# Fixing the first four experts, keeping the split tokens in natural order, and moving the end of the sort into the first experts

## The chip, the cores and the metric

The kernel runs on one core of a Trainium2 chip. The metric is the time of one execution on the device in microseconds (us), the median of several runs. The engines of the core are PE (matrix products; PEld is its weight load, which overlaps the products), DVE, ACT and POOL (elementwise work), and SP, which here only issues transfers (DMA).

## The reference, cut to what matters

The reference is a whole block with two attentions and a mixture of experts, followed by a second block. Only the mixture is touched. Each of 512 tokens picks one of 4 groups, then 2 of the 8 experts of that group; every one of the 32 experts has its own three weight matrices.

```python
pg = jax.nn.softmax((hf @ wg + bg), axis=-1)
gsel = jnp.argmax(pg, axis=-1)
le = (hf @ we + be).reshape(n, N_GROUPS, EXPERTS_PER_GROUP)
le = jnp.take_along_axis(le, gsel[:, None, None], axis=1)[:, 0]
p_top, e_loc = lax.top_k(jax.nn.softmax(le, axis=-1), TOP_K)
gate = pg_sel[:, None] * p_top / jnp.sum(p_top, axis=-1, keepdims=True)
...
def expert_block(args):
    xb, e = args
    return (jax.nn.silu(xb @ w1[e]) * (xb @ w3[e])) @ w2[e]
...
out = jnp.zeros((n + 1, d), ys.dtype).at[tok_buf].add(ys)[:n]
```

d is 1024, the hidden width of an expert 512. One expert's weights are 3 x 2 MB in fp32, all of them 192 MB.

## The kernel before, in words

`phase2` does the output projection of the attention, the routing and the experts. The 512 tokens are four tiles (t = 0 to 3) of 128 rows.

**Routing.** `project` adds the projection to the residual `x`. For each tile, `logits` transposes `x` on PE and multiplies by the router's weights, `route` finds group and experts by a chain of small DVE instructions, and a product with `Ab` gives each token its rank within its expert. `onehot` turns ranks into a selection matrix `G`. `spread` writes the normalized tile as a sum of two rounded parts, `hi` (ACT) and `lo` (DVE), in fp32r; both are written permuted, so that the 128 columns that one product needs stand side by side. For tile 2 `lo` is computed on POOL.

**Order of the experts.** `sort` orders the experts by how many tokens they have; its `key` puts those with a mark of 65536 first. `idi` holds the sorted experts' numbers, `rp` the ranks and gates in that order. `STEPS` says how many experts each of 12 steps takes: 2 (with 64 rows each) or 4 (with 32 rows). Experts 0 and 1 are marked, so that step 0 is known when the program is built.

**Steps.** A gather multiplies `hi` and `lo` (the stationary operand, as `hv(t, b)[:, k * P:(k + 1) * P]`) by `G` and leaves the chosen tokens transposed in `xg`, in 8 blocks k. The first gather, for step 0, stands at line 1141. `expert_step` then does w1 and w3 in halves of 4 blocks, the gate, four transposes and w2; between its parts `todo[0]` to `todo[4]` run what belongs to other steps: gathers ahead (line 1006), the preparation of gates (`slots`), and `back`, which adds the finished step's result to `x` (the combine, line 1304).

**Weights.** The pool behind `slot()` has 14 buffers of 1 MB (`NW2`). A step of two experts takes 12 of them, four for each matrix, a step of four experts 24. SP issues the loads strictly in program order; a load waits until the products that read its buffer's last content are done, and from step 1 on it waits for `value_load`, which reads the experts' numbers from `idi` (line 868). Experts that have more tokens than rows are taken by a loop after the steps; its body does not run with these inputs. The work after the experts (`project2`) begins when the last combine is done.

Of the kernel before, what the change touches and what calls it, by code (L numbers as in the profile page):

```python
# [10 lines left out]
F32 = mybir.dt.float32  # L11
# [3 lines left out]
AF = mybir.ActivationFunctionType  # L15
# [14 lines left out]
def constants():  # L30

    c = {}
    q = np.arange(P)
    c["sq"] = np.concatenate([
        np.eye(P),
        np.where(q[None, :] < q[:, None], 0.0, NEG),
        q[:, None] < q[None, :],
    ], axis=1).astype(np.float32)

    tok = np.arange(S)  # L40
    f = np.float32(10000.0) ** (-np.arange(8, dtype=np.float32) / np.float32(8))
# [12 lines left out]

    e = np.arange(32)
    c["order"] = np.concatenate([31 - e + 65536 * (e < 2), PLACES, np.repeat([128 // n for n in STEPS], STEPS)])
    c["rows"] = np.concatenate([
        q[:, None] % 32 == e[None], (q % 32)[:, None],
        q[:, None] // 32 == np.arange(4)[None], q[:, None] // 64 == np.arange(2)[None],
    ], axis=1).astype(np.float32)  # L60
    c["tok1"] = (q[:, None] + P * np.arange(NT)[None, :] + 1).astype(np.float32)

    rel = np.arange(640) - 127 - 384
    n = np.abs(rel)
    nf = np.maximum(n, 1).astype(np.float32)
    large = 8 + (np.log(nf / np.float32(8)) / np.float32(math.log(128 / 8)) * np.float32(8)).astype(np.int32)
    large = np.minimum(large, 15)
    bucket = np.where(rel > 0, 16, 0) + np.where(n < 8, n, large)
    oh = np.zeros((32, 640), np.float32)
    oh[bucket, np.arange(640)] = 1.0  # L70
    c["onehot"] = oh
    return c
# [35 lines left out]

STEPS = (2, 4, 2, 2, 4, 2, 2, 4, 2, 2, 4, 2)
_small, _large = iter(range(16, 32)), iter(range(16))
PLACES = np.array([next(_small if n == 4 else _large) for n in STEPS for _ in range(n)])

# [1 line left out]
class K:  # L116
# [733 lines left out]
    def phase2(self, p2):  # L850
# [13 lines left out]
        def weights(i):  # L864

            n = STEPS[i]
            if i:
                es = [nc.sync.value_load(idi[:, p:p + 1], min_val=0, max_val=E - 1) for p in range(first[i], first[i + 1])]
            else:
                es = range(n)  # L870
            out = []
            for nm in ("w1", "w3", "w2"):
                if i:
                    src = [I[nm][0, bass.ds(e, 1)].rearrange("o (p k) n -> p (o k) n", p=P) for e in es]
                else:
                    src = [I[nm][0, e].rearrange("(p k) n -> p k n", p=P) for e in es]
# [17 lines left out]
        ws = self.wos  # L894
        hs = [None, None]
        hv = lambda t, b: hs[t // 2][b].rearrange("q a s -> q (a s)")[:, (t % 2) * D:(t % 2 + 1) * D]
        Ab = T([P, NT, E], "Ab", BF16)
        st = T([P, NT, 84], "st")

# [77 lines left out]
        def spread(t, rstd):  # L977

            if hs[t // 2] is None:
                hs[t // 2] = self.half(1 - t // 2)  # L980
            hi, lo = hv(t, 0), hv(t, 1)
            xk = self.x[:, t, :].rearrange("q (p k) -> q k p", k=KD)
            r = lambda b: b.rearrange("q (k p) -> q k p", k=KD)
            sc.activation(r(hi), xk, AF.Copy, scale=rstd)
            if t == 2:
                for h in (slice(0, KD // 2), slice(KD // 2, KD)):
                    xs = T([P, S], "pm").rearrange("q (k p) -> q k p", p=P)
                    gp.tensor_scalar(xs, xk[:, h], rstd, None, ALU.mult)
                    gp.tensor_tensor(r(lo)[:, h], xs, r(hi)[:, h].bitcast(F32), ALU.subtract)
            else:  # L990
                stt(r(lo), xk, rstd, r(hi).bitcast(F32), ALU.mult, ALU.subtract)

        def onehot(G, steps, t, src):

# [7 lines left out]
        def gather(xg, G, ks, m):  # L1002
            for k in ks:
                ps = self.psum()
                for i, (b, t) in enumerate((b, t) for t in range(NT) for b in range(2)):
                    te.matmul(ps[:, :m], hv(t, b)[:, k * P:(k + 1) * P], G[:, t, :m],
                              start=i == 0, stop=i == 2 * NT - 1)
                scaled(xg[:, k, :m], ps[:, :m], k)

# [71 lines left out]

        rstd = [None] * NT
        new_G = lambda: T([P, NT, 4 * CAP], "G", F32R)
        G = new_G()
        for i, (t, n) in enumerate(((0, 0), (0, 1), (1, 0), (1, 1), (2, 1), (3, 1), (2, 0), (3, 0))):
            project(t, n)
            if i in (1, 3, 6, 7):
                rstd[t] = self.rsqrt1(1.0 / D, st[:, t, 0:1], st[:, t, 1:2])
                ps = logits(t)
                route(t, ps, rstd[t])  # L1090
                onehot(G, (0,), t, rt)
        order = sort()
        next(order)
        for t in range(NT):
            spread(t, rstd[t])

        def table():

# [31 lines left out]


        NB, NX = 18, 8
        new_xg = lambda: self.xg().rearrange("p a (b s) -> p (a b) s", b=2)
        xg = new_xg()
        acs = [self.accum() for _ in range(4)] + [self.psum() for _ in range(3)]
        acs.append(self.po.tile([P, 512], F32, tag="o", name=self.name("o")))
        part = lambda k: acs[k][:, :P]
        for t in range(NT):
            for k in range(KD):
                for b in range(2):  # L1140
                    te.matmul(part(k), hv(t, b)[:, k * P:(k + 1) * P], G[:, t, :P], start=t + b == 0, stop=t + b == NT)
        for k in range(KD):
            scaled(xg[:, k, :P], part(k), k)
        next(order)
        _, gc = slots(G, (0,), rt)
        combine, nx, got, over = [], None, [], []
        N = len(STEPS)
        for i in range(N):
            todo = [[] for _ in range(5)]
            j = (i + 1) % 2  # L1150
            ahead = [g for g in (i + 2 - j, i + 3 - j) if g < N] if i else (1, 2)
            if i == 0 or (j == 0 and ahead):
                nx = new_xg()
                G = new_G()
                for t in range(NT):
                    onehot(G, ahead, t, rp)
                sl = slots(G, ahead, rp)
                todo[1].append(lambda s=sl: next(s))
                got = []
                todo[3].append(lambda s=sl, g=got: g.append(next(s)))  # L1160
            if ahead:
                m = P * len(ahead)
                if i == 0:
                    todo[0].append(lambda x=nx, g=G, m=m: gather(x, g, range(4), m))
                k0 = 4 * j
                todo[2].append(lambda x=nx, g=G, k=k0, m=m: gather(x, g, (k, k + 1), m))
                todo[3].append(lambda x=nx, g=G, k=k0, m=m: gather(x, g, (k + 2, k + 3), m))
            for p, f in zip((0, 1), combine):
                todo[p].append(f)
            if i == 1:  # L1170
# [5 lines left out]
            if last:  # L1176
                more = self.next_weights()
                todo[4].append(self.split_next)
            c = 0 if i == 0 else j
            combine = self.expert_step(T, xg, c * P, STEPS[i], P, w1, w3, w2, gc[:, 0, c:c + 1], gc[:, 1, c:c + 1],  # L1180
                                       iota, todo)
            if last:
                for f in combine:
                    f()
            if j and not last:
                xg = nx
                gc, = got

        tab, tabi = over
        _, (nb,) = nc.values_load_multi_w_load_instructions(tabi[:, NB:], min_val=0, max_val=NB)  # L1190
        with tc.For_i(0, nb, 1) as ib:
# [26 lines left out]
            for k in range(KD):  # L1218
                ps = self.psum()
                for i, (b, t) in enumerate((b, t) for t in range(NT) for b in range(2)):  # L1220
                    te.matmul(ps[:, :CAP], hv(t, b)[:, k * P:(k + 1) * P], G[:, t, :CAP],
                              start=i == 0, stop=i == 2 * NT - 1)
# [3 lines left out]
            for f in self.expert_step(T, xg, 0, 1, CAP, w1, w3, w2, gc[:, 0, :1], gc[:, 1, :1], iota):  # L1226
                f()


# [19 lines left out]
        self.split_next = split_next  # L1249
        return self.free  # L1250

    def expert_step(self, T, xg, c0, ne, m, w1, w3, w2, gate, tok, iota, todo=()):


        nc = self.nc
# [8 lines left out]
        for i, (w, a) in enumerate(zip((w1, w3), ac)):  # L1264
# [10 lines left out]
        v.scalar_tensor_tensor(h[:m], ac[1][:m], gate[:m], h[:m], ALU.mult, ALU.mult)  # L1275
        between(2)
        ps = self.psum()
        for k in range(4):
# [5 lines left out]
        v.tensor_scalar(pm[:m], iota[:m], tok[:m], None, ALU.is_equal)  # L1284
        y = [self.accum() for _ in range(2)]
        kp = 4 // len(w2)
        for k in range(4):
# [559 lines left out]
```

## Time and profile before

| what | value |
|---|---|
| time, median of 3 runs | 1518.69 us (1517.68 to 1523.06) |
| profiled execution | 1516.21 us, span 1514.4 us |
| PE busy | 1432.1 us, 95% of the span |
| PEld / DVE / ACT / POOL busy | 962.0 / 720.6 / 502.1 / 123.8 us |
| granted clock of PE, mean | 0.971 of full speed |
| moved by DMA | 303.81 MB, mean 201 GB/s |

The shares are means over stages with different limits: routing and first gather end at about 377 us, the twelve steps run to about 857 us, and there the transfers matter; before and after, the weights are small against the products. [...]

### The profile page before, as it was taken

To read this page: it belongs to the slowest core of one execution; us is meant where nothing else is said; L and a number is where in the kernel's file an instruction comes from. 1 tells how busy PE (TensorE), PEld (TensorE's weight loads), DVE (VectorE), ACT (ScalarE), POOL (GpSimd) and SP (SyncE) were. 2 spreads that over 40 slices of the span, in tenths; PEclk is the share of its full clock that TensorE was granted. 3 is DMA by queue.
4 is the path that set the end of the run, shared out by engine and by line. 5 is a ranking of instruction groups with operands and counts; after the bars stand their busy time and mean duration, and the time that the engine had idled before them with its cause. 6 is when DMAs were issued, how large, how long until landed. Compare 5 with 4: busy or idle time off the path is not lost. (4 is left out here: it accounts for less than half of the span.)

```text
span 1514.4 us, 20068 instructions
## 1 busy us (share of the span) xinstructions
PE 1432.1 (95%) x7322; PEld 962.0 (64%) x7322; DVE 720.6 (48%) x1907; ACT 502.1 (33%) x1031; POOL 123.8 (8%) x145
## 2 busy tenths in 40 slices
PE   8999999998988999999999698999989999999997
PEld 6776657587434434433433387888878888888886
DVE  5465487867224322321222486667575333325356
ACT  5344454644101000100000454556445222224351
POOL 0012122301000000000000230110011000000000
PEclk9999997996999999999999899999999999999999
DMA  7647761061999999999999601110032331223211
GB/s 249 204 154 216 248 219 56 1 256 78 343 405 420 413 409 421 415 409 418 418 409 416 250 33 41 57 56 2 16 137 99 111 112 57 83 84 109 101 42 56
DMA packets 91957, 303.81 MB, mean 201 GB/s; under 512 B 6432, under 2 KB 12208, under 8 KB 79440
## 3 DMA queue, kind: packets, MB, share of 16 engines
q1 hardware_dynamic: 90016, 299.02, 51.4%
q0 software_dynamic: 1712, 3.35, 0.8%
q8 instruction: 59, 0.97, 0.3%
q14 instruction: 42, 0.34, 0.1%
q10 hardware_dynamic: 128, 0.13, 0.0%
HBM read 297.82 MB, written 2.56 MB: 198 GB/s over the span
## 5 line engine op out<-in xcount | busy, mean ns | idle before, releaser
L1268 PE MATMUL acc<-w,xg 128*32 128x512 f32 (+1 forms) x1024 | 216.1, 601 | 3.9 <-DMA w<-in_w_dram 3.9
L229 DVE TENSOR_TENSOR wlo<-w,whi 128x512 fp32r<-128x512 f32 (+3 forms) x161 | 104.0, 648 | 207.7 <-ACT whi L228 190.3
L228 ACT ACTIVATE whi<-w 128x512 fp32r<-128x512 f32 (+2 forms) x177 | 104.7, 596 | 219.0 <-PE o L236 86.2
L1268 PEld LDWEIGHTS acc<-w,xg 128*32 128x32 f32 (+1 forms) x1024 | 56.9, 124 | 122.8 <-issue 98.4
L1290 PE MATMUL acc<-w,hid 128*32 128x512 f32 (+1 forms) x512 | 120.8, 607 | 0.8 <-ACT hid L1281 0.7
L235 PE MATMUL acc<-whi,hi 128*128 128x512 f32 x280 | 112.4, 404 | 0.4 <-ACT hid L726 0.4
L236 PE MATMUL acc<-wlo,hi 128*128 128x512 f32 x280 | 112.3, 401 | 0.0
L237 PE MATMUL acc<-whi,lo 128*128 128x512 f32 x280 | 111.4, 398 | 0.0
L235 PE MATMUL acc<-hi,whi 128*128 128x512 f32 (+1 forms) x272 | 100.2, 372 | 2.8 <-ACT hi L1702 2.4
L237 PE MATMUL acc<-hi,wlo 128*128 128x512 f32 (+1 forms) x272 | 100.9, 372 | 0.6 <-POOL wlo L229 0.6
L236 PE MATMUL acc<-lo,whi 128*128 128x512 f32 (+1 forms) x272 | 101.0, 372 | 0.3 <-DVE lo L1703 0.2
L1275 DVE SCALAR_TENSOR_TENSOR hid<-acc,gc,hid 128x512 f32<-128x512 f32 x12 | 9.0, 751 | 158.1 <-PE acc L1268 142.6
L1290 PEld LDWEIGHTS acc<-w,hid 128*32 128x32 f32 (+1 forms) x512 | 37.8, 125 | 72.7 <-issue 59.3
L1305 DVE TENSOR_TENSOR x_sb<-ps,x_sb 128x512 f32<-128x512 f32 x96 | 60.6, 684 | 22.9 <-PE ps L1304 22.7
L235 PE MATMUL ps<-hi,whi 128*128 128x512 f32 x160 | 64.0, 400 | 0.0
L237 PE MATMUL ps<-hi,wlo 128*128 128x512 f32 x160 | 63.5, 397 | 0.0
L236 PE MATMUL ps<-lo,whi 128*128 128x512 f32 x160 | 63.5, 397 | 0.0
L235 PEld LDWEIGHTS acc<-whi,hi 128*128 128x128 f32 x280 | 52.9, 190 | 15.3 <-issue 1.4
L236 PEld LDWEIGHTS acc<-wlo,hi 128*128 128x128 f32 x280 | 53.0, 189 | 13.6 <-issue 1.8
L237 PEld LDWEIGHTS acc<-whi,lo 128*128 128x128 f32 x280 | 52.9, 189 | 12.9 <-issue 0.5
L235 PEld LDWEIGHTS acc<-hi,whi 128*128 128x128 f32 x272 | 51.0, 189 | 14.9 <-ACT hi L1702 3.0
L229 DVE TENSOR_TENSOR hid<-acc,hid 128x512 fp32r<-128x512 f32 x12 | 8.3, 691 | 106.8 <-PE acc L1290 95.7
(506 smaller groups left out, 2838.2 us busy)
## 6 DMA issues: line engine op xcount, KB each, us to landing
w<-in_w_dram SPq DMA_DIRECT2D x96, 1024.0 KB
w<-in_w_dram SPq DMA_DIRECT2D x192, 512.0 KB
w<-in_w_ada_dram SPq DMA_DIRECT2D x12, 2048.0 KB
w<-in_w_in_dram SPq DMA_DIRECT2D x5, 2048.0 KB
w<-in_w_gate_dram SPq DMA_DIRECT2D x5, 2048.0 KB
w<-in_w_up_dram SPq DMA_DIRECT2D x5, 2048.0 KB
w<-in_w_down_dram SPq DMA_DIRECT2D x4, 2048.0 KB
w<-in_w_o_dram SPq DMA_DIRECT2D x2, 2048.0 KB
```

The source lines that it names most:

```text
L228: nc.scalar.activation(hi, src, AF.Copy)
L229: (eng or nc.vector).tensor_tensor(lo, src, hi.bitcast(F32), ALU.subtract)
L235: mm(out, a[0], b[0], start=first, stop=False)
L236: mm(out, a[0], b[1], start=False, stop=False)
L237: mm(out, a[1], b[0], start=False, stop=last)
L1268: te.matmul(a[r, :], xg[:, k, c0 + r.start:c0 + r.stop], w[k // kp][e][:, k % kp, :], start=k == 0, stop=k == KD - 1)
L1275: v.scalar_tensor_tensor(h[:m], ac[1][:m], gate[:m], h[:m], ALU.mult, ALU.mult)
L1290: te.matmul(y[n][r, :], hT[:, k, r], w2[k // kp][e][:, k % kp, n * 512:n * 512 + 512], start=k == 0, stop=k == 3)
L1305: v.tensor_tensor(self.x[:, t, cs], ps, self.x[:, t, cs], ALU.add)
```

## The change

Four things change. Experts 0 to 3 are marked, in order, and `STEPS` begins with two steps of two experts (2, 2, 4, 2, 4, 2, 2, 4, 2, 4, 2, 2); the loads of steps 0 and 1 no longer read `idi`. `spread` writes `hi` and `lo` in the tokens' natural order, for all tiles on ACT and DVE, and the products read them with a stride of 8 elements (`hk`). The first gather collects its 8 blocks in two PSUM banks instead of eight buffers. The second half of `sort`, the gates of step 0 and the selection for steps 1 and 2 run inside step 0, in `todo[0]`, after the first half of w1.

```diff
-    c["order"] = np.concatenate([31 - e + 65536 * (e < 2), PLACES, ...
+    c["order"] = np.concatenate([31 - e + 65536 * np.maximum(4 - e, 0), PLACES, ...
-STEPS = (2, 4, 2, 2, 4, 2, 2, 4, 2, 2, 4, 2)
+STEPS = (2, 2, 4, 2, 4, 2, 2, 4, 2, 4, 2, 2)
...
-            if i:
+            if i > 1:
                 es = [nc.sync.value_load(idi[:, p:p + 1], ...
...
+        hk = lambda t, b, k: hv(t, b)[:, k::KD]
...
-            sc.activation(r(hi), xk, AF.Copy, scale=rstd)
-            if t == 2:
-                for h in (slice(0, KD // 2), slice(KD // 2, KD)):
...
-                    gp.tensor_scalar(xs, xk[:, h], rstd, None, ALU.mult)
-                    gp.tensor_tensor(r(lo)[:, h], xs, r(hi)[:, h].bitcast(F32), ALU.subtract)
-            else:
-                stt(r(lo), xk, rstd, r(hi).bitcast(F32), ALU.mult, ALU.subtract)
+            sc.activation(hi, self.x[:, t, :], AF.Copy, scale=rstd)
+            stt(lo, self.x[:, t, :], rstd, hi.bitcast(F32), ALU.mult, ALU.subtract)
...
-                    te.matmul(ps[:, :m], hv(t, b)[:, k * P:(k + 1) * P], G[:, t, :m],
+                    te.matmul(ps[:, :m], hk(t, b, k), G[:, t, :m],
...
         next(order)
+        xg = new_xg()
+        acs = [self.accum() for _ in range(2)]
+        part = [a.rearrange("p (k s) -> p k s", k=4) for a in acs]
         for t in range(NT):
-            spread(t, rstd[t])
+            for k in range(KD):
+                for b in range(2):
+                    te.matmul(part[k // 4][:, k % 4], hk(t, b, k), G[:, t, :P], ...
+        for i in range(2):
+            tt(xg[:, k, :P], part[i], g2[:, k, None].to_broadcast([P, 4, P]), ALU.mult)
...
-        next(order)
-        _, gc = slots(G, (0,), rt)
...
+                def ordered(nx=(nx := new_xg()), m=2 * P):
+                    next(s0)
+                    next(order)
+                    G = new_G()
+                    for t in range(NT):
+                        onehot(G, ahead, t, rp)
+                    sl = slots(G, ahead, rp)
+                    gc = next(s0)
+                    todo[1] += [lambda: gather(nx, G, range(4), m), lambda: next(sl)]
+                    todo[2].append(lambda: gather(nx, G, (4, 5), m))
+                    todo[3] += [lambda: gather(nx, G, (6, 7), m), lambda: pair.append(next(sl))]
...
+                todo[0].append(ordered)
```

On the queue of SP, the loads of steps 0 and 1 (`w`, 1 MB each) and the read of the sorted numbers (`idi`), before:

```order
L203 DMA w_2900<-in_w_dram 128x2048
L203 DMA w_2902<-in_w_dram 128x2048
L868 TENSOR_LOAD idi_2906
L868 ISA x2
...
L888 DMA w_3695<-in_w_dram 128x1024
```

and now:

```order
L203 DMA w_2900<-in_w_dram 128x2048
L203 DMA w_2902<-in_w_dram 128x2048
L203 DMA w_3642<-in_w_dram 128x2048
L203 DMA w_3644<-in_w_dram 128x2048
L203 DMA w_3646<-in_w_dram 128x2048
...
L868 TENSOR_LOAD idi_2906
```

The twelve loads of step 1 moved ahead of the read of `idi` (w_3648 to w_3664 are left out above). w_3642 and w_3644 take the two buffers that step 0 leaves free and wait for no product.

On PE, between the last rank (line 962, now 963, product with `Ab` of tile 3) and the first product of the experts (`acc<-w,xg`), the end before, where `bd` and `rs` belong to the sort and to the gates of step 0:

```order
L1141 MATMUL o_3356<-G_2911,lo_696_3338 128x128
L1073 MATMUL ps_3429<-bd_2909,small_383 128x32
L1073 MATMUL ps_3429<-bd_2909,col_3321 128x32
L1078 MATMUL ps_3434<-bd_2909,hid_3329 128x64 x4
L1027 MATMUL ps_3444<-G_2911,rs_3440 5x128 x4
L1268 MATMUL acc_3470<-w_2880,xg_3348 64x512
```

and now:

```order
L1097 MATMUL acc_3345<-G_2911,lo_691_3317 128x128
L1279 MATMUL acc_3413<-w_2880,xg_3343 64x512
...
L1020 MATMUL ps_3427<-G_2911,rs_3423 5x128 x4
L1066 MATMUL ps_3434<-bd_2909,small_383 128x32
L1066 MATMUL ps_3434<-bd_2909,col_3333 128x32
L1071 MATMUL ps_3439<-bd_2909,hid_3341 128x64 x4
L1026 MATMUL ps_3454<-cst,row_3432 128x5
L1279 MATMUL acc_3413<-w_2884,xg_3343 64x512
```

The products of the sort's end and of the gates moved behind the first 8 products of w1 (the row with w_2880 stands for them). Between the last rank and the experts 34 products of the first gather stood before; now it is 26, the last 16 of them of tile 3.

On DVE, in the routing of tiles 2 and 3, `lo` is line 991 before and 984 now; before, tile 2's stands on POOL and one stands here:

```order
L941 TENSOR_REDUCE st_2905<-st_2905 128x1
L959 SCALAR_TENSOR_TENSOR st_2905<-desc_386,st_2905 128x8
L960 TENSOR_TENSOR Ab_2904<-st_2905 128x32
L991 SCALAR_TENSOR_TENSOR lo_696_3338<-x_sb,r_y_3242,hi_695_3337 128x1024
L963 SCALAR_TENSOR_TENSOR rt_2879<-ps_3169,Ab_2904 128x32
L970 SCALAR_TENSOR_TENSOR st_2905<-st_2905 128x1
L934 SCALAR_TENSOR_TENSOR L_3276<-ps_3253,r_y_3242,flat_381 128x36
```

and now there are two:

```order
L952 TENSOR_REDUCE st_2905<-sel_3204 128x8
L940 TENSOR_REDUCE st_2905<-st_2905 128x1
L984 SCALAR_TENSOR_TENSOR lo_691_3317<-x_sb,r_y_3164,hi_690_3316 128x1024
L941 SCALAR_TENSOR_TENSOR st_2905<-st_2905,desc_386 128x8
...
L950 TENSOR_TENSOR sel_3288<-L_3282,st_2905 128x32
L984 SCALAR_TENSOR_TENSOR lo_691_3317<-x_sb,r_y_3248,hi_690_3316 128x1024
...
L952 TENSOR_REDUCE st_2905<-sel_3288 128x8
L940 TENSOR_REDUCE st_2905<-st_2905 128x1
```

Tile 2's `lo` moved from POOL to the middle of tile 2's routing here, and tile 3's `lo` from behind tile 2's `Ab` (line 960) into the middle of tile 3's routing (its `sel` is sel_3288).

## Rows read from the trace of the kernel before

**Rows 1.** Waits of the DMA-issuing queue of SP, 320 to 400 us: total, times, longest
```profile
SPq L868 <- DVE left L1100: 46.4, 1, 46.4
```

**Rows 2.** Stretches: length, busy PE, PEld, DVE, ACT, POOL (instructions), granted clock, DMA share, GB/s
```profile
353.00:378.00 25.00, 20.35 (x102) 19.30 (x103) 17.19 (x77) 7.02 (x16) 5.22 (x4) 0.54 0.00 1
395.00:410.00 15.00, 15.00 (x88) 7.85 (x86) 4.74 (x24) 1.92 (x4) 0.00 (x0) 1.00 1.01 387
410.00:450.00 40.00, 35.73 (x231) 14.84 (x231) 10.66 (x35) 3.71 (x7) 1.53 (x3) 0.96 1.02 396
450.00:840.00 390.00, 372.24 (x1767) 147.86 (x1758) 101.33 (x226) 32.68 (x61) 0.18 (x1) 1.00 1.02 415
```

**Rows 3.** DMA queues, 375 to 442 us: packets, MB moved, share
```profile
q1 hardware_dynamic: 6341, 23.11, 90.1%
```

**Rows 4.** Timeline of PE, first step of experts: start, length, line
```profile
377.46 1.97 PE L1268 MATMUL acc<-w,xg 128*64 128x512 f32 x2
...
379.56 4.95 PE L1268 MATMUL acc<-w,xg 128*64 128x512 f32 x14
...
388.39 7.09 PE L1268 MATMUL acc<-w,xg 128*64 128x512 f32 x32
...
395.98 3.65 PE L1268 MATMUL acc<-w,xg 128*64 128x512 f32 x16
...
404.43 7.09 PE L1290 MATMUL acc<-w,hid 128*64 128x512 f32 x32
...
415.02 2.25 PE L1304 MATMUL ps<-hid,pm 128*128 128x512 f32 x8
```

**Rows 5.** Timeline of PE, routing and first gather, with idle time before and its releaser
```profile
345.56 0.38 PE L917 MATMUL ps<-cst,x_sb 128*128 128x128 f32 x1 [1.98 <-DVE x_sb L907]
...
350.40 0.28 PE L1141 MATMUL acc<-G,lo 128*128 128x128 f32 x1
350.51 0.27 PE L1141 MATMUL acc<-G,hi 128*128 128x128 f32 x1
...
359.25 0.18 PE L962 MATMUL ps<-Ab,cb 128*128 128x32 bf16 x1 [2.23 <-DVE Ab L960]
...
365.98 0.18 PE L962 MATMUL ps<-Ab,cb 128*128 128x32 bf16 x1 [0.90 <-DVE Ab L960]
...
370.51 0.41 PE L1141 MATMUL acc<-G,hi 128*128 128x128 f32 x1
...
373.71 0.41 PE L1141 MATMUL o<-G,lo 128*128 128x128 f32 x1
```

**Rows 6.** Costliest groups of ACT by shape: busy, mean ns | idle before
```profile
L984 ACT ACTIVATE hi<-x_sb,r_y 128x1024 fp32r<-128x1024 f32 x4 | 8.9, 2237 | 4.2 <-DVE r_y L269 2.6 <-PE acc L237 1.6
...
L1683 ACT ACTIVATE w<-x_sb 128x1024 f32<-128x1024 f32 x4 | 4.2, 1045 | 3.5 <-POOL w L229 3.5
```

**Rows 7.** Costliest groups of DVE by shape: busy, mean ns | idle before
```profile
L991 DVE SCALAR_TENSOR_TENSOR lo<-x_sb,r_y,hi 128x1024 fp32r<-128x1024 f32 x3 | 6.5, 2180 | 1.2 <-ACT hi L984 1.2
...
L639 DVE SCALAR_TENSOR_TENSOR sbk<-sbk,st,sbq 128x512 f32<-128x512 f32 x4 | 3.0, 750 | 0.0
```

**Rows 8.** Timeline of DVE, routing of the tiles: start, length, line
```profile
333.30 0.23 DVE L940 SCALAR_TENSOR_TENSOR st<-st,desc 128x8 f32<-128x8 f32 x1
...
351.50 1.20 DVE L940 SCALAR_TENSOR_TENSOR st<-L,st,desc 128x4 f32<-128x4 f32 x1
...
357.58 0.93 DVE L940 SCALAR_TENSOR_TENSOR st<-st,desc 128x8 f32<-128x8 f32 x1
```

**Rows 9.** Timeline of POOL, 350 to 360 us
```profile
351.44 2.12 POOL L988 TENSOR_SCALAR pm<-x_sb,r_y 128x512 f32<-128x512 f32 x1 [27.48 <-ACT pm L909]
```

**Rows 10.** Weight loads by line, ns min/median/max
```profile
L528 PEld LDWEIGHTS ps<-cst,nsq x32: 138/141/231, 199.8 to 324.2; 128*128 128x128 f32 x32
...
L917 PEld LDWEIGHTS ps<-cst,x_sb x32: 185/193/370, 324.3 to 355.9; 128*128 128x128 f32 x32
...
L1006 PEld LDWEIGHTS ps<-G,lo x192: 186/188/194, 384.5 to 800.5; 128*128 128x128 f32 x192
```

More of the change, by code (lines that the diff above doesn't have):

```diff
@@ L55, in constants @@
     e = np.arange(32)
-    c["order"] = np.concatenate([31 - e + 65536 * (e < 2), PLACES, np.repeat([128 // n for n in STEPS], STEPS)])
+    c["order"] = np.concatenate([31 - e + 65536 * np.maximum(4 - e, 0), PLACES, np.repeat([128 // n for n in STEPS], STEPS)])
     c["rows"] = np.concatenate([
@@ L866, in weights @@
             n = STEPS[i]
-            if i:
+            if i > 1:
                 es = [nc.sync.value_load(idi[:, p:p + 1], min_val=0, max_val=E - 1) for p in range(first[i], first[i + 1])]
             else:
-                es = range(n)
+                es = range(first[i], first[i + 1])
             out = []
             for nm in ("w1", "w3", "w2"):
-                if i:
+                if i > 1:
                     src = [I[nm][0, bass.ds(e, 1)].rearrange("o (p k) n -> p (o k) n", p=P) for e in es]
@@ L981, in spread @@
             hi, lo = hv(t, 0), hv(t, 1)
-            xk = self.x[:, t, :].rearrange("q (p k) -> q k p", k=KD)
-            r = lambda b: b.rearrange("q (k p) -> q k p", k=KD)
-            sc.activation(r(hi), xk, AF.Copy, scale=rstd)
-            if t == 2:
-                for h in (slice(0, KD // 2), slice(KD // 2, KD)):
-                    xs = T([P, S], "pm").rearrange("q (k p) -> q k p", p=P)
-                    gp.tensor_scalar(xs, xk[:, h], rstd, None, ALU.mult)
-                    gp.tensor_tensor(r(lo)[:, h], xs, r(hi)[:, h].bitcast(F32), ALU.subtract)
-            else:
-                stt(r(lo), xk, rstd, r(hi).bitcast(F32), ALU.mult, ALU.subtract)
+            sc.activation(hi, self.x[:, t, :], AF.Copy, scale=rstd)
+            stt(lo, self.x[:, t, :], rstd, hi.bitcast(F32), ALU.mult, ALU.subtract)
         def onehot(G, steps, t, src):
@@ L1083, in phase2 @@
         new_G = lambda: T([P, NT, 4 * CAP], "G", F32R)
+        new_xg = lambda: self.xg().rearrange("p a (b s) -> p (a b) s", b=2)
         G = new_G()
@@ L1091, in phase2 @@
                 onehot(G, (0,), t, rt)
+            if i in (5, 7):
+                for u in (0, 1) if i == 5 else (2, 3):
+                    spread(u, rstd[u])
         order = sort()
         next(order)
+        xg = new_xg()
+        acs = [self.accum() for _ in range(2)]
+        part = [a.rearrange("p (k s) -> p k s", k=4) for a in acs]
         for t in range(NT):
-            spread(t, rstd[t])
+            for k in range(KD):
+                for b in range(2):
+                    te.matmul(part[k // 4][:, k % 4], hk(t, b, k), G[:, t, :P], start=t + b + k % 4 == 0,
+                              stop=t + b == NT and k % 4 == 3)
+        for i in range(2):
+            k = slice(4 * i, 4 * i + 4)
+            tt(xg[:, k, :P], part[i], g2[:, k, None].to_broadcast([P, 4, P]), ALU.mult)
         def table():
@@ L1132, in phase2 @@
         NB, NX = 18, 8
[L1133 to L1143, printed above, removed]
-        next(order)
-        _, gc = slots(G, (0,), rt)
-        combine, nx, got, over = [], None, [], []
+        sl = slots(G, (0,), rt)
+        got = []
+        combine, nx, over = [], None, []
         N = len(STEPS)
@@ L1151, in phase2 @@
             ahead = [g for g in (i + 2 - j, i + 3 - j) if g < N] if i else (1, 2)
[L1152 to L1167, printed above, removed]
+            if i == 0:
+                s0 = sl
+                def ordered(nx=(nx := new_xg()), m=2 * P):
[9 more added lines that the diff above has]
+                    todo[3] += [lambda: gather(nx, G, (6, 7), m), lambda: pair.append(next(sl))]
+                    got.append(gc)
+                pair = []
+                todo[0].append(ordered)
+            else:
+                if j == 0 and ahead:
+                    nx = new_xg()
+                    G = new_G()
+                    for t in range(NT):
+                        onehot(G, ahead, t, rp)
+                    sl = slots(G, ahead, rp)
+                    todo[1].append(lambda s=sl: next(s))
+                    pair = []
+                    todo[3].append(lambda s=sl, g=pair: g.append(next(s)))
+                if ahead:
+                    m = P * len(ahead)
+                    k0 = 4 * j
+                    todo[2].append(lambda x=nx, g=G, k=k0, m=m: gather(x, g, (k, k + 1), m))
+                    todo[3].append(lambda x=nx, g=G, k=k0, m=m: gather(x, g, (k + 2, k + 3), m))
             for p, f in zip((0, 1), combine):
@@ L1179, in phase2 @@
             c = 0 if i == 0 else j
-            combine = self.expert_step(T, xg, c * P, STEPS[i], P, w1, w3, w2, gc[:, 0, c:c + 1], gc[:, 1, c:c + 1],
-                                       iota, todo)
+            combine = self.expert_step(T, xg, c * P, STEPS[i], P, w1, w3, w2,
+                                       lambda q, g=got, c=c: g[0][:, q, c:c + 1], iota, todo)
             if last:
@@ L1185, in phase2 @@
             if j and not last:
-                xg = nx
-                gc, = got
+                xg, got = nx, pair
         tab, tabi = over
@@ L1220, in phase2 @@
                 for i, (b, t) in enumerate((b, t) for t in range(NT) for b in range(2)):
-                    te.matmul(ps[:, :CAP], hv(t, b)[:, k * P:(k + 1) * P], G[:, t, :CAP],
+                    te.matmul(ps[:, :CAP], hk(t, b, k), G[:, t, :CAP],
                               start=i == 0, stop=i == 2 * NT - 1)
@@ L1225, in phase2 @@
                                       more[2 * i:2 * i + 2]) for i, nm in enumerate(("w1", "w3", "w2")))
-            for f in self.expert_step(T, xg, 0, 1, CAP, w1, w3, w2, gc[:, 0, :1], gc[:, 1, :1], iota):
+            for f in self.expert_step(T, xg, 0, 1, CAP, w1, w3, w2, lambda q: gc[:, q, :1], iota):
                 f()
@@ L1250, in next_weights, with expert_step @@
         return self.free
-    def expert_step(self, T, xg, c0, ne, m, w1, w3, w2, gate, tok, iota, todo=()):
+    def expert_step(self, T, xg, c0, ne, m, w1, w3, w2, col, iota, todo=()):
         nc = self.nc
@@ L1274, in expert_step @@
                 sc.activation(h[:m], ac[0][:m], AF.Silu)
-        v.scalar_tensor_tensor(h[:m], ac[1][:m], gate[:m], h[:m], ALU.mult, ALU.mult)
+        v.scalar_tensor_tensor(h[:m], ac[1][:m], col(0)[:m], h[:m], ALU.mult, ALU.mult)
         between(2)
@@ L1283, in expert_step @@
         pm = T([P, S], "pm", F32R)
-        v.tensor_scalar(pm[:m], iota[:m], tok[:m], None, ALU.is_equal)
+        v.tensor_scalar(pm[:m], iota[:m], col(1)[:m], None, ALU.is_equal)
         y = [self.accum() for _ in range(2)]
```

## The prediction

> **What bounds the kernel now.** First the table of stretches: in the steady part of the experts, 450 to 840 us, the DMA share is 1.02 at 415 GB/s, from 395 us on it is 1.01 and more, and between 353 and 378 us it is 0.00 [rows 2]. PE is busy throughout the steps too, but 192 MB of weights have to pass, and a step may only be multiplied when they are there. So the stage is paced by bytes, and what counts is how early the transfers run without a gap. A slot of 1 MB (1.049 million bytes) takes 2.53 us at 415 GB/s.
>
> Next the wait that holds the transfers: the queue of SP stands 46.4 us at line 868, for DVE [rows 1]: what it reads there are the sorted experts' numbers. Twelve slots hold step 0, two stay empty meanwhile. What comes after depends on releases: slots come free as step 0's products are done with them. By 442 us 23.11 MB have moved, 22.0 slots [rows 3].
>
> Last the timeline of PE, for when those releases happen. Its first expert product starts at 377.46. The rows count each fp32 product as two, so that half a projection (8 products of the code) has 16. The first half of w1 ends at 384.51, after 7.05 us at half clock; later halves take 3.55 (7.09 for two, 3.65 for one), and w2 begins at 404.43 [rows 4]. [...]
>
> **The change, part by part.**
>
> *Four fixed experts.* Step 1's twelve loads no longer wait for the sort. Its first two take the two empty slots, early and at no price, since DMA is idle. The other ten wait for step 0's products anyway. SP reads `idi` behind them; by then the sort has ended, so no wait replaces the 46.4 us. The same bytes move in all.
>
> *The split.* Contiguous writing of 128x1024 by ACT takes 1.05 us where the strided one takes 2.24 [rows 6]. For `lo` on DVE no contiguous 128x1024 stands in the trace; 0.75 for 128x512 doubles to at most 1.50, and I take 1.28 for an operation with three streams, between that and ACT's 1.05, against 2.18 now [rows 7]. Three of them save 2.7 us; a wait of 1.2 for `hi` [rows 7] shrinks or goes. The fourth, tile 2's, comes to DVE from POOL: +1.3. In return the small routing instructions are undisturbed: while POOL computes (four instructions from 351.44 on, 5.22 us [rows 2, 9]), one of 0.23 us takes 1.20, seven of them, the last at 357.58, some 4.4 us more in sum than undisturbed [rows 8]. Together -7.0. Not all of it is on the path: at 345.56 PE waits 1.98 for DVE, which is the nearest lower bound, and before the two ranks at 359.25 and 365.98 it waits 2.23 and 0.90 [rows 5]. I take 5 of 2 to 7: last rank at 361.0 instead of 365.98.
>
> *First gather in two banks.* Behind the last rank 26 products stand, before 34. At half clock they start .213 us apart (3.20 us between the first and last of 16) [rows 5]: 5.5 us. The evictions, two instead of eight, end with the second bank; I give .4 between gather and experts. So the first expert product stands at 361.0 + 5.5 + .4 = 366.9, 10.5 earlier.
>
> *The sort's end.* Between the last gather product (373.71 + .41) and 377.46 it costs 3.3 us now [rows 4, 5]. Inside step 0 DVE can start it while PE does the first half of w1, which waits for nothing of it; PE's small products and the gates stand behind that half, in the way of the next. At most all 3.3 remain, at least the half's worth; I take 2.5, nearer to the whole, since PE's and DVE's pieces wait for each other in turn and the two evictions come first on DVE. The gathers for steps 1 and 2 stand later now and have the second half of w1 and first of w3 to hide the selection.
>
> *Sum for step 0.* Half w1 at half clock 7.05: 373.9. Sort's end: 376.4. The same rest as before, 404.43 - 384.51 = 19.9: w2 begins at 396.3, its first half is done at 399.9 instead of 404.43 + 3.55 = 408.0. That is 8.1 us, of 10.5, the sort's end having eaten the difference. The last of step 0's slots come free at 403.4.
>
> *Step 1 is now a step of two experts.* PE needs for it 4 halves of 3.55, two combine halves of 2.25 [rows 4], .6 for gates, and 4.8 for gathers, gate and transposes (395.98 + 3.65 to 404.43 in step 0): 24.1. Its w2 begins at 427.5 and ends at about 434.6. It uses weights of which 2 MB arrived early and the rest behind the releases; they land before their products or little after. Its slots are then free for the step of four experts, and the transfers run without a gap from there.
>
> *What it is worth.* I count slots at one mark, pair by pair: 5.06 us each, none before its release. New: the early pair; step 0's releases at 373.9, 380, 383.5, 391.7, 399.9 and 403.4 (halves, sort's end and gathers in their order) bring 14 slots by 410.0, and step 1's six, of which the last two at 431.1 and 434.6 are the only ones that DMA waits for, 26 by 441.3. Before, 22.0 had moved by 442 [rows 3]. 26 less 22.0, and the .3 that 442 adds, are 4.3 slots, 10.9 us. The same bookkeeping on the old program (two slots from 378, releases at 384.5, 391.9, 395.5, 399.6, 408.0, 411.5 [rows 4]: 14 by 418.1, then no gap) gives 23.4 by 442, 1.4 too quick, 3.6 us: left is 7.3. The release of w2 in step 0, 8.1 earlier, gives another figure of the same kind. I take **8 us**. As all later steps wait for bytes, nothing returns it: they move the same total, and steps of two and four only change places (a two-expert step needs 12 slots, 30.4 us of DMA, against the 31 us of PE just counted, and between them stand steps of four with 60.7 us of DMA).
>
> The profiled execution, 1516.2 us with 1514.4 of span, becomes 1508.2; it was 2.5 faster than the median of the runs, 1518.69, so the median to expect is **1511**.
>
> **The strided weight loads** are the one part that speaks against this. `hk` reads with a stride of 8 elements. The trace holds no strided load in fp32r. The nearest: transposes that load with a stride of 8 take 193 ns, contiguous ones 141, and contiguous fp32r loads 188 already [rows 10], so a strided fp32r load may take no longer, or 1.37 times, or twice. At full clock products start .11 apart (350.40, 350.51) [rows 5], less than a load takes; loads lie beside products, and only what exceeds them counts. I take nothing; the bounds are 0 and .107 us per load at full clock, .213 at half.
>
> [...]
>
> **Rivals.**
>
> *A, slower: strided loads pace the gathers.* If a load takes twice, 26 first-gather products get .213 each (5.5 us), the 64 of step 0's gathers .096 (6.1) and 32 of step 1 as much (3.1): 14.7 us, and up to 5 more before the rank, where the products compete with routing. Against a gain of 8 that is 7 to 12 slower: 1525 to 1530. Later gathers lie beside transfers and cost nothing until PE becomes the bound. It decides at .054 us per load (8 us over 26 loads counted twice for the half clock, and 96). For it: 193 against 141. Against: 188 for fp32r loads that are contiguous.
>
> [...]
>
> *C, no change: two steps of two swallow it.* Step 1 was a step of four, 24 slots for DMA under one long step of PE. Now PE has to finish two short ones before transfers can run ahead; if its wait for step 1's weights, or for a gather, costs some 5 us in 400 to 440, 0 to 4 us of gain remain: 1516. For it: PE was busy 35.73 of 40 us at 410 to 450 with the DMA share already 1.02 [rows 2], so that there was no gap of DMA to close after 395; the gain must come from before.
>
> *That the change does nothing* of what it says is excluded by the order of the instructions; what it moves is worth 8 us by release times.
>
> **How the numbers follow.** The forecast, a gain of 4 to 12, gets .48, B .14, C .15, A .23. A measurement of this kernel tells differences from about 0.5%, 7.6 us; the forecast lies on that bound, so half of its chance and all of B's count as faster, .38; two thirds of A's as slower, .15; the remainder, .47, as no difference. The range, 1504 to 1526, takes in B's time and the nearer end of A, and leaves out what is beyond both. The likeliest case's own is 1507 to 1515.
>
> **What would show it.** Right: DMA busy briefly before 353 us with two slots; no 46 us at line 868; `hi` at 1.05 and `lo` near 1.28; no stretched DVE instructions at 351 to 358; the last rank near 361, the first expert product near 367, the first half of w2 in step 0 done near 400, step 1's w2 at 427 to 435; from there a DMA share of 1. Wrong: first-gather products that start .4 apart at half clock or gathers of steps at .21 at full clock, with loads near 0.3 us (A); a granted clock well over 0.54 in 353 to 378 (B); a DMA share under 0.9 between 400 and 440 us with PE busy (C); or a step of the later stage that now ends on PE.

## The result, and the profile after

The changed kernel takes 1528.31 us (median of 4 runs, 1527.29 to 1529.89), the kernel before 1518.21 beside it: a ratio of 1.0065, 95% interval 1.0046 to 1.0085. It is 10 us slower where 8 us faster was forecast; 1528.3 lies above the range and inside rival A's 1525 to 1530. The profiled execution took 1527.29, with a span of 1525.5.

The stretches, as in [rows 2]:

```profile
353.00:378.00 25.00, 25.00 (x121) 20.48 (x123) 11.77 (x65) 3.36 (x8) 0.00 (x0) 0.61 0.10 29
378.00:395.00 17.00, 17.00 (x78) 10.83 (x76) 3.18 (x17) 3.20 (x5) 0.00 (x0) 1.00 0.84 339
395.00:410.00 15.00, 15.00 (x70) 10.39 (x66) 4.11 (x21) 1.55 (x3) 0.00 (x0) 1.00 0.44 152
410.00:450.00 40.00, 40.00 (x189) 20.21 (x189) 11.77 (x37) 4.80 (x9) 1.69 (x3) 1.00 0.95 364
450.00:840.00 390.00, 375.57 (x1759) 175.38 (x1753) 100.04 (x224) 30.92 (x58) 0.00 (x0) 0.98 1.02 414
```

From 353 to 410 us PE has no idle time at all now (25.00 of 25.00, before 20.35), and still DMA stands still for more than half of 395 to 410: 0.44, before 1.01. At 410 the transfers are still a little ahead, since more had passed before that gap: 14.14 MB of weights and other loads since 340, before 13.87. At 480 they are behind, 40.80 against 42.14; the queue of the weights in the changed kernel, 340 to 480 us (packets, MB, share):

```profile
q1 hardware_dynamic: 9003, 40.80, 74.5%
```

What PE does meanwhile in the changed kernel, with the columns of [rows 4] and [rows 5]:

```profile
363.50 0.25 PE L963 MATMUL ps<-Ab,cb 128*128 128x32 bf16 x1
...
370.10 4.75 PE L1279 MATMUL acc<-w,xg 128*64 128x512 f32 x16
...
376.85 7.09 PE L1279 MATMUL acc<-w,xg 128*64 128x512 f32 x32
...
384.22 0.41 PE L999 MATMUL ps<-G,lo 128*128 128x256 f32 x1
384.46 0.40 PE L999 MATMUL ps<-G,hi 128*128 128x256 f32 x1
384.70 0.40 PE L999 MATMUL ps<-G,lo 128*128 128x256 f32 x1
...
404.44 7.09 PE L1301 MATMUL acc<-w,hid 128*64 128x512 f32 x32
```

The last rank is at 363.50 (365.98 before), the first expert product at 370.10 (377.46 before), 7.4 us earlier. But the gather products of step 0 start .24 apart where they stood .12 apart before, and w2 begins at 404.44, before at 404.43. The same products in the kernel before:

```profile
384.66 0.28 PE L1006 MATMUL ps<-G,lo 128*128 128x256 f32 x1
384.77 0.28 PE L1006 MATMUL ps<-G,hi 128*128 128x256 f32 x1
384.89 0.28 PE L1006 MATMUL ps<-G,lo 128*128 128x256 f32 x1
```

All that was won ahead of the experts is gone there. The weight loads of these products in the changed kernel, as in [rows 10]:

```profile
L999 PEld LDWEIGHTS ps<-G,lo x192: 312/338/343, 384.1 to 821.2; 128*128 128x128 f32 x192
```

338 ns instead of 188 (`hi` 337). That is near rival A's double, and it holds for all 384 gather products. The other side of the split came as costed: `hi` and `lo` as in [rows 6] and [rows 7], now contiguous, and no routing instruction stretched by POOL: the `st` of line 941 takes at most .23, where that of line 940 took up to 1.20 before [rows 8].

```profile
L983 ACT ACTIVATE hi<-x_sb,r_y 128x1024 fp32r<-128x1024 f32 x4 | 4.6, 1142 | 1.6 <-PE acc L237 1.6
```

```profile
L984 DVE SCALAR_TENSOR_TENSOR lo<-x_sb,r_y,hi 128x1024 fp32r<-128x1024 f32 x4 | 5.1, 1280 | 0.0
```

At the other end the last combine is done at 867.0, before at 856.6: 10.4 of the 11.1 us that the span is longer. At 840 the transfers are only 1.3 MB behind (189.82 against 191.12 since 340), 3.1 us. So a second loss lies between the arrival of the bytes and PE. The last two steps on PE's timeline: the start of the combine before them, w2 and the combine of the last but one, the last w2, and the last product of the combine:

```profile
790.82 1.89 PE L1315 MATMUL ps<-hid,pm 128*128 128x512 f32 x6
...
821.66 9.44 PE L1301 MATMUL acc<-w,hid 128*64 128x512 f32 x32
831.03 1.89 PE L1315 MATMUL ps<-hid,pm 128*128 128x512 f32 x6
...
852.92 8.83 PE L1301 MATMUL acc<-w,hid 128*64 128x512 f32 x32 [0.69 <-ACT hid L1292]
...
866.62 0.39 PE L1315 MATMUL ps<-ylo,pm 128*128 128x512 f32 x1
```

### The profile page after: what moved, and what is told of

Its sections match the earlier page's. It is cut to its first block, busy times and chain, and to the rows that moved or that the text cites. A ratio compares the mean times of both kernels' runs of the same rounds, so it can differ in the third digit from the quotient of the medians.

```text
span 1525.5 us, 20028 instructions
## 1 busy us (share of the span) xinstructions
PE 1455.7 (95%) x7322; PEld 1006.9 (66%) x7322; DVE 713.8 (47%) x1906; ACT 496.6 (33%) x1027; POOL 117.4 (8%) x141
## 5 line engine op out<-in xcount | busy, mean ns | idle before, releaser
L1279 PE MATMUL acc<-w,xg 128*32 128x512 f32 (+1 forms) x1024 | 205.2, 598 | 1.2 <-DMA w<-in_w_dram 1.2
L1301 PE MATMUL acc<-w,hid 128*32 128x512 f32 (+1 forms) x512 | 108.7, 626 | 0.7 <-ACT hid L1292 0.7
L999 PE MATMUL ps<-G,hi 128*128 128x256 f32 (+1 forms) x192 | 80.1, 417 | 0.0
L999 PE MATMUL ps<-G,lo 128*128 128x256 f32 (+1 forms) x192 | 79.0, 411 | 0.0
L999 PEld LDWEIGHTS ps<-G,hi 128*128 128x128 f32 x192 | 64.2, 334 | 11.3 <-issue 7.4
L999 PEld LDWEIGHTS ps<-G,lo 128*128 128x128 f32 x192 | 64.6, 336 | 8.2 <-issue 8.2
L1005 ACT ACTIVATE xg<-ps,small 128x256 f32<-128x256 f32 (+1 forms) x24 | 11.0, 457 | 175.2 <-PE ps L999 175.2
```

Of the source, the lines that this page charges most:

```text
L999: te.matmul(ps[:, :m], hk(t, b, k), G[:, t, :m], start=i == 0, stop=i == 2 * NT - 1)
L1005: sc.activation(dst, ps, AF.Copy, scale=g2[:, k:k + 1])
L1279: te.matmul(a[r, :], xg[:, k, c0 + r.start:c0 + r.stop], w[k // kp][e][:, k % kp, :], start=k == 0, stop=k == KD - 1)
L1301: te.matmul(y[n][r, :], hT[:, k, r], w2[k // kp][e][:, k % kp, n * 512:n * 512 + 512], start=k == 0, stop=k == 3)
```

## The experiments

All were timed with the kernel before on the same chip, in 6 to 12 runs each. Single executions of one kernel scatter by some 5 us to either side, with the mean granted clock (0.961 to 0.977), so the ratios with their intervals count. Marks on a timeline are those of one execution, and they carry the start of its routing: the first transpose of `x` stands at 324.42 before, at 324.99 in the changed kernel, and between 324.3 and 329.1 in all.

Theory L: the strided loads are the whole loss. Rival T: most of it is made by the new order of the steps, since two steps of two experts at the end leave PE behind DMA.

**Loads contiguous again.** `hi` and `lo` written permuted, all by ACT and DVE:

```diff
-        hk = lambda t, b, k: hv(t, b)[:, k::KD]
+        hk = lambda t, b, k: hv(t, b)[:, k * P:(k + 1) * P]
...
-            sc.activation(hi, self.x[:, t, :], AF.Copy, scale=rstd)
-            stt(lo, self.x[:, t, :], rstd, hi.bitcast(F32), ALU.mult, ALU.subtract)
+            sc.activation(r(hi), xk, AF.Copy, scale=rstd)
+            stt(r(lo), xk, rstd, r(hi).bitcast(F32), ALU.mult, ALU.subtract)
```

> The changed kernel with hi and lo written permuted again (by ACT and DVE for all tiles), so that every weight load of the gathers is contiguous; all else as changed. Theory L, the strided loads are the whole loss: gather products start .12 apart instead of .24, w2 of step 0 begins near 397 to 399 instead of 404.4 (64 products by .12 are 7.7 us, less some 3 us for the slower writing), DMA has no gap to 410, and the kernel ends at 1508 to 1513. Rival T, most of the loss is made at the end, where two steps of two experts follow each other and PE needs longer for them (40.2 us for the last but one in the changed kernel) than DMA for 24 slots: then w2 of step 0 is earlier too, but the last steps stay on PE with 36 and 31 us, and the kernel is at 1517 to 1521.

Measured: 1512.67 us, ratio 0.9967 (0.9955 to 0.9980). Loads 188 ns. 15.6 us come back by this edit alone; L holds by the time, T's 1517 to 1521 does not. Where it comes back was not as expected: w2 of step 0 begins at 405.65 in the profile, not at 397 to 399. The routing of this execution starts 3.9 later than the changed kernel's (first transpose at 328.93), so w2 is 2.7 earlier than there; of the 7.7 us of 64 products, the slower writing takes back 5.2, by which the first expert product is later (379.22 against 370.10, less the 3.9). By 480 us 2.71 MB more have moved than in the changed kernel (43.51 against 40.80), 6.5 us; the rest of the 15.6 comes behind that.

**Another order of the steps**, with strided loads, and with contiguous ones:

```diff
-STEPS = (2, 2, 4, 2, 4, 2, 2, 4, 2, 4, 2, 2)
+STEPS = (2, 2, 4, 2, 2, 4, 2, 4, 2, 2, 4, 2)
```

> The changed kernel with strided loads, and only the order of later steps changed, so that the last three take 2, 4, 2 experts as in the kernel before, and not 4, 2, 2. Theory L: no change, 1526 to 1529, the gathers cost what they cost. Rival T: the last step no longer starts on PE's time but on DMA's, which is 1.3 MB or 3.1 us late against the kernel before; the kernel ends 6 to 8 us earlier, 1520 to 1523.

> Both at once: contiguous loads and the last steps 2, 4, 2. Theory L: as the permuted one alone, 1508 to 1513, and no gain from the order. Rival T: the end follows DMA, which is now earlier than in the kernel before by the gain of the first steps: 1509 to 1513, some 7 us under the permuted one alone.

Measured: 1526.20 us, ratio 1.0068 (1.0044 to 1.0093), and 1512.24, ratio 0.9964 (0.9947 to 0.9981). Neither differs from its partner beyond the intervals. T falls as the main cause, but the marks show what the order does with strided loads: it moves the second loss. In the changed kernel 90.46 MB had passed by 600 us, in this one only 87.97, a loss of 6 us, at the place where its pair of two-expert steps now stands.

**The strided loads in the kernel before**, with natural order for `hi` and `lo` (all by ACT and DVE), and nothing else of the change:

```diff
...
-te.matmul(ps[:, :m], hv(t, b)[:, k * P:(k + 1) * P], G[:, t, :m],
+te.matmul(ps[:, :m], hv(t, b)[:, k::KD], G[:, t, :m],
...
```

> The kernel before with one part of the change: hi and lo in natural order by ACT and DVE, and strided loads in all gathers. Theory L: the writing saves 3 to 5 us ahead of the experts, the 64 gather products of step 0 and the 32 of step 1 cost 11.6 more; w2 of step 0 begins 3 to 5 us later, and the kernel is at 1521 to 1525. Rival T: the end goes by DMA since the last steps are 2, 4, 2, and the later gathers cost nothing; the loss is what DMA is late after step 0, 0 to 3 us: 1518 to 1521.

Measured: 1528.01 us, ratio 1.0078 (1.0058 to 1.0099). Slower than both theories had it. w2 of step 0 began at 410.4, by 480 us 2.09 MB were missing (5.0 us at 415 GB/s), by 600 us 5.17 (12.4 us), and the last combine ended 12.2 later. 600 us is behind its first pair of two-expert steps, and the share of DMA falls there (0.84 from 540 to 560 us). So the later gathers aren't hidden everywhere: at that pair PE is the bound. At its second pair (600 to 660 us) the share is 1.02, and nothing is lost.

**The distance of the stride.** With groups of 2 or of 4 elements kept together the loads have that stride; DVE writes `lo` in 4 or 2 pieces. For 2:

```diff
-        hk = lambda t, b, k: hv(t, b)[:, k::KD]
+        hk = lambda t, b, k: hv(t, b)[:, k // 2 * 256 + k % 2:k // 2 * 256 + 256:2]
...
+            vw = lambda a: a.rearrange("q (p h l) -> q h p l", h=4, l=2)
+            r = lambda a: a.rearrange("q (h p l) -> q h p l", h=4, l=2)
+            sc.activation(r(hi), vw(self.x[:, t, :]), AF.Copy, scale=rstd)
+            for h in range(4):
+                stt(r(lo)[:, h], vw(self.x[:, t, :])[:, h], rstd, r(hi)[:, h].bitcast(F32), ...)
```

> The changed kernel with another layout of hi and lo: element pairs stay together, so that the weight loads of the gathers have a stride of 2 elements (8 bytes) and not 8; DVE writes lo in four pieces of 128x256. Theory L2, a load pays for every element that isn't next to the last: loads near 337 ns and products .24 apart as with stride 8, and 1524 to 1530. [...]

> The same with groups of four: stride of 4 elements (16 bytes), lo in two pieces of 128x512. Theory L2: .24 apart, as with strides of 2 and 8, 1524 to 1530. [...] If the price grows with the distance instead, it lies between: .18 or so apart and 1515 to 1521.

Measured: stride 2 takes 1510.04 us, ratio 0.9951 (0.9932 to 0.9970), stride 4 takes 1525.75, ratio 1.0047 (1.0031 to 1.0063). The loads, stride 2 first:

```profile
L1002 PEld LDWEIGHTS ps<-G,lo x192: 193/198/201, 382.6 to 805.4; 128*128 128x128 f32 x192
```

```profile
L1002 PEld LDWEIGHTS ps<-G,lo x192: 307/330/339, 383.6 to 820.1; 128*128 128x128 f32 x192
```

198 ns against 330: pairs cost nearly nothing (188 contiguous), and with a stride of 16 bytes the price is nearly that of 32 (338). L2, a price for every element that isn't next to the last, falls, since with a stride of 2 neither its 337 ns nor its 1524 to 1530 came. A price that grows with the distance falls too: 1525.75 is not within its 1515 to 1521, and the load takes 132 ns more from 2 to 4 elements, 8 more from 4 to 8. The price sets in between 8 and 16 bytes, with 140 to 150 ns for each load over the contiguous one; what makes it isn't shown. With stride 2 the other steps of the prediction can be read without the loads' price; its last rank, first half of w1 and w2 of step 0 on PE, and its weights' queue from 340 to 480 us:

```profile
361.70 0.18 PE L963 MATMUL ps<-Ab,cb 128*128 128x32 bf16 x1
...
367.82 5.60 PE L1282 MATMUL acc<-w,xg 128*64 128x512 f32 x16
...
395.34 7.09 PE L1304 MATMUL acc<-w,hid 128*64 128x512 f32 x32
```

```profile
q1 hardware_dynamic: 9750, 45.82, 82.6%
```

**Half of the loads.** `hi` with stride 8, `lo` with stride 2 (b is 0 for `hi`):

```diff
-hk = lambda t, b, k: hv(t, b)[:, k::KD]
+hk = lambda t, b, k: hv(t, b)[:, k // 2 * 256 + k % 2:k // 2 * 256 + 256:2] if b else hv(t, b)[:, k::KD]
```

> hi in natural order with a stride of 8, lo in pairs with a stride of 2, so that half of the loads are strided. If every strided load costs its own .12 us, the loss is half of the 18 us between 1510.0 and 1528.3: 1517 to 1521, and starts of products alternate between .12 and .24. If PE can hide a long load behind the short one next to it, less: 1511 to 1515.

Measured: 1518.43 us, ratio 1.0003 (0.9984 to 1.0022), the middle of 1510.0 and 1528.3 (1519.2) within a microsecond. Starts on PE:

```profile
386.76 0.29 PE L1001 MATMUL ps<-G,lo 128*128 128x256 f32 x1
386.88 0.41 PE L1001 MATMUL ps<-G,hi 128*128 128x256 f32 x1
387.13 0.28 PE L1001 MATMUL ps<-G,lo 128*128 128x256 f32 x1
387.25 0.40 PE L1001 MATMUL ps<-G,hi 128*128 128x256 f32 x1
```

The long and the short distance take turns, .12 and .25: each strided load costs its own, and the short one beside it hides nothing.

**The parts of the change by themselves.** First the marks, the loads of experts 0 to 3 and the order of steps, on the kernel before:

```diff
-31 - e + 65536 * (e < 2)
+31 - e + 65536 * np.maximum(4 - e, 0)
...
-STEPS = (2, 4, 2, 2, 4, 2, 2, 4, 2, 2, 4, 2)
+STEPS = (2, 2, 4, 2, 4, 2, 2, 4, 2, 4, 2, 2)
...
-            if i:
+            if i > 1:
```

> The kernel before with the marks for experts 0 to 3, their loads and the new order of steps alone; the split, the first gather and the sort's end as before. By the prediction's bookkeeping, two slots come early but all others still wait for the same releases of step 0, so that most of the gain of 8 is not here: 1514 to 1518. Rival P, PE is the bound where two steps of two experts follow each other, and there are now three such pairs, one at the end: 0 to 4 us slower, 1518 to 1522.

Then the sort's end back ahead of the experts, in the kernel with contiguous loads:

```diff
-                todo[0].append(ordered)
+                ordered()
```

> The changed kernel with permuted split (contiguous loads) and the sort's end, gates and selection back ahead of the first expert product. By the prediction: the place inside step 0 saves .8 us of 3.3 and the slots of the first half of w1 come free earlier, so 1 to 3 us slower than the permuted one, 1513.5 to 1516. Rival: it costs the same wherever it stands, since DMA waits for the later releases: no difference, 1511 to 1513.5.

The split alone on the kernel before, with the layout of stride 2 shown above:

> The kernel before with the split alone: hi and lo in pairs on ACT and DVE for all tiles, loads with a stride of 2. The prediction put the split at 5 us of the 10.5 that the first expert product comes earlier: if that is so and reaches the end by the same share as the rest (8 of 10.5), 1513 to 1515.5. Rival: without the early pair of slots the releases of step 0 carry all of it: 1511 to 1513. Second rival: it stays on DVE, and nothing comes of it: 1517 to 1519.

And the first gather in eight buffers again, in the kernel with a stride of 2:

```diff
-te.matmul(part[k // 4][:, k % 4], hk(t, b, k), G[:, t, :P], start=t + b + k % 4 == 0, ...
+te.matmul(part(k), hk(t, b, k), G[:, t, :P], start=t + b == 0, stop=t + b == NT)
...
+        for k in range(KD):
+            scaled(xg[:, k, :P], part(k), k)
```

> The kernel with a stride of 2, and the first gather in eight buffers with eight evictions again. By the prediction it loses what two banks saved, 34 products against 26 behind the last rank at .213 (1.7 us) and the evictions: 1511 to 1514. Rival: the evictions stand beside products of the next block, so that there is no difference: 1509 to 1511.

| kernel | us | ratio to before | to compare with |
|---|---|---|---|
| fixed experts and order alone | 1515.07 | 0.9983 (0.9965 to 1.0001) | 1: unclear |
| sort's end ahead, contiguous loads | 1515.58 | 0.9981 (0.9964 to 0.9998) | 0.9967 with it inside: unclear |
| split alone, stride 2 | 1511.35 | 0.9954 (0.9934 to 0.9973) | 1: 7 us faster |
| eight buffers, stride 2 | 1511.14 | 0.9952 (0.9933 to 0.9970) | 0.9951 with two banks: no difference seen |

The split in pairs alone brings 7.0 us and all four parts with it 7.4, with intervals of some 3 us to either side of each; of what was expected for it, the first rival's 1511 to 1513 came. Its first expert product stands at 372.4 and its w2 of step 0 at 399.2, 5.1 and 5.2 earlier than before. What the other three add is within the scatter.

**The version that follows**, stride 2 and the other order of steps:

> Loads with a stride of 2 and the last steps 2, 4, 2. If two steps of two at the end still cost what the bytes at 840 us and the end show (the permuted one had 1.4 MB, 3.3 us, in hand there and ended no earlier than the kernel before), 1506 to 1508.5; if the order of steps is worth nothing without the strided loads, 1509 to 1511, as the one with a stride of 2 alone (1510.0).

Measured: 1508.96 us, ratio 0.9937 (0.9912 to 0.9962): the fastest of all, 9.6 us under the kernel before. Whether the order has a part in it is open; the interval takes in 0.9951.

## Why the prediction was wrong, step by step

**The step that failed** is the price of the strided loads: "I take nothing". It rested on the row with 188 ns for a contiguous fp32r load, so near to the 193 of strided transposes that the stride seemed paid already. But those transposes are fp32 and these loads fp32r, with a contiguous price of their own; nearer was the step from 141 to 193 that one kind of load takes with the stride. Even that would give only 240 to 258 ns. The measured step is 188 to 338, and .12 us of PE for each product at full clock; against the kernel with a stride of 2 it makes 18.3 us (1528.3 and 1510.0). The prediction gave rival A, which has this cause, .23.

**Rival A had the cause and the time, by another sum.** It put 5.5 us on the first gather, since it let the price double with the half clock. The strided products start .24 apart at a granted clock of .50 (358 to 370 us) and at 1.00 (384 to 391) alike, and contiguous ones stood .213 apart at half clock [rows 5], so the 26 cost .7. The 64 of step 0 and 32 of step 1 cost .12 each, 11.5 us, for which A had 9.2. Against the kernel with stride 2 the changed one lacks 5.02 MB by 480 us (40.80 against 45.82), 12.1 us. That this is so near to .7 and 11.5 is in part luck: the last rank, too, is 1.8 later (363.50 against 361.70), as A had it for the products that compete with the routing, and the first half of w1 is .9 shorter. That A's 1525 to 1530 came true is luck in part as well, since it had no loss behind step 1.

**"Later gathers lie beside transfers and cost nothing"**, which stands in rival A ("until PE becomes the bound") and which the forecast needs without that condition, failed at the end. A two-expert step needs 30.4 us of DMA and, by the prediction, 31 of PE, "and between them stand steps of four". In the order of the changed kernel the sixth and seventh step and the last two stand side by side. At the former nothing is lost: what the changed kernel lacks against stride 2 stays at 5.00 MB by 600 us (90.46 against 95.46) and 4.69 by 840 (189.82 against 194.51). In the last two it is. From the start of the combine at 790.82 to that of the next at 831.03 PE needed 40.2, and 34.0 with stride 2:

```profile
778.75 1.89 PE L1318 MATMUL ps<-hid,pm 128*128 128x512 f32 x6
...
805.70 7.14 PE L1304 MATMUL acc<-w,hid 128*64 128x512 f32 x32
812.76 1.89 PE L1318 MATMUL ps<-hid,pm 128*128 128x512 f32 x6
...
834.65 7.14 PE L1304 MATMUL acc<-w,hid 128*64 128x512 f32 x32 [0.69 <-ACT hid L1295]
```

In these two executions the changed kernel's last combine ends 20.0 later (867.0 and 847.0), of which 12.1 were made by 480 us. Of the other 7.9, 3.9 are the 32 strided products of the last step but one, 2.3 its w2, which took 9.44 instead of 7.14 at a granted clock of 0.73 (821 to 831 us), and 1.7 the last w2, which took 8.83 instead of 7.14 at 0.83 (852 to 862). The kernel before has 8.83 for its last w2, too, so that dip comes without strided loads. The one of 9.44 may come of them: with a stride of 4 this w2 took 8.37, and in the six other kernels with this order of steps 7.14. But each is one execution, and w2 of step 0 took 7.09 behind the same kind of gather, so this is not shown.

**The rest of the sum held in the main**, as the kernel with a stride of 2 shows:

- `hi` took 1.14 and `lo` 1.28 in natural order, forecast 1.05 and 1.28; in pairs 1.29 and four times .48. No POOL, no stretched instruction. So the rank came near its forecast though `lo` in pairs takes 1.9 and not 1.28.
- Last rank 361.7 (forecast 361.0), first expert product 367.8 (366.9), w2 of step 0 at 395.3 (396.3). Between them errors cancel: the first half of w1 took 5.60, not 7.05, at a granted clock of 0.64, where before it was 0.66, so that the half clock was not all that made it long; what else did stays open. The sort's end takes 2.0 in the changed kernel, from the end of the first half of w1 at 374.85 to 376.85 (2.5).
- By 442 us 30.17 MB had moved since 340, before 26.35: 3.82 MB or 9.2 us, forecast 7.3 to 10.9. The end: 1510.0, forecast 1511.

**Its parts were perhaps shared out wrongly.** The sum of the four is right, but by the medians the split alone gives almost all of it, where the prediction saw the early pair of slots and the shorter gather at work beside it. It forecast 5 us for the split at the first expert product, and that came (5.1); that as much or more would reach the end without the other parts was not foreseen. That fixed experts alone bring little, as the bookkeeping of releases has it, fits 1515.07. By 840 us the kernel with all four parts is 1.10 MB, 2.7 us, ahead of the one with the split alone (194.51 and 193.41), but at the end the medians are only 1.3 apart, and the intervals can't tell either from nothing. So that nothing of a gain is returned later isn't shown, and that the total agrees may be luck.

The chances and the range count B, a granted clock well over 0.54 in 353 to 378, with .14 and a time of 1504. No run shows that time, and what the runs show of the clock is worth less: in the changed kernel it was .50 through the gather (358 to 370), 0.61 in 353 to 378, and .76 in the first half of w1, which took 4.75, against .64 and 5.60 with stride 2, some .9 us. Rival C (a gap of DMA in 400 to 440 with PE busy) came as its sign said, with a share of .85 there and .44 in 395 to 410, but for A's reason: with stride 2 the share is 1.02 in 400 to 440, and .83 in 395 to 410.

## What to carry to other kernels

Where an edit trades a strided write for a strided read, count who reads: here seven writes of a tile become about a microsecond shorter each, and 384 weight loads pay .12 us, 46 us on PE, of which 18 reached the end. A price that is missing from the trace should be taken from the step that the nearest kind makes with the same edit (141 to 193), not from a total that happens to be near (188), and then be measured, since here even that step was a third of the true one (52 and 150). And look for the middle layout: pairs of neighbours gave a cheaper write (1.29 on ACT and 1.9 on DVE, against 2.24 and 2.18) and the cheap load at once.

A stage that is paced by bytes hides engine work only while each step's engine time stays under its transfer time, or while there are transfers in hand; with 34 us of PE against 30.4 of DMA the short steps at the end had nothing left to hide in, though the average share of DMA was 1.02 from 450 to 840 us.

## What the runs showed of the hardware

- Weight loads of 128x128 in fp32r: 188 ns contiguous, 198 with a stride of 2 elements, 330 with 4, 338 with 8. Products of 256 columns start .12 apart with the first two and some .24 with the others.
- The pace of products with strided loads (8 elements) doesn't follow the granted clock: .24 apart at .50 and at 1.00. Contiguous ones are .213 and .12 apart, so the stride costs .03 at the lower level and .12 at the higher.
- fp32 transposes with a stride of 8 pay 52 ns (193 against 141), fp32r loads 150. Why they differ stays open.
